# A hybrid decoder layer on one core: loading the input, placing the query work, and ordering seven products

## The chip, the core and the metric

The kernel runs on one NeuronCore of a Trainium2 chip. The engines are TensorE (PE in the profile, with its weight loads as PEld), VectorE (DVE), ScalarE (ACT), GpSimd (POOL) and SyncE (SP, which here only issues DMAs). The metric is the device time of one execution in microseconds; the median of three runs counts.

## The reference, cut to what matters

```python
xn = rmsnorm(x, norm1_w)
proj = xn @ w_in                    # q | k,v of three branches | gates | xr | yr | merge gates
q = rope_partial(rmsnorm(q, q_norm_w), t)
o_nsa = nsa_mixer(q, ...)           # compressed, selected and window attention
xc = conv_b + sum(xp[:, j:j + S] * conv_w[j] for j in range(4))
o_lru = rg_lru(xc) * gelu(yr)       # gates, scan over the sequence
merged = sigmoid(g_a) * (o_nsa @ w_nsa_up) + sigmoid(g_b) * (o_lru @ w_lru_up)
h = x + merged @ w_o
out = h + square(relu(rmsnorm(h, norm2_w) @ w_ff1)) @ w_ff2
```

The sequence has 1024 tokens, the model width is 1024, the hidden layer of the last two products is 4096 wide. All data are float32.

## The kernel before

Every float32 product is made of three passes with the operands split into a high part (`h`, by ACT) and a low part (`l` = value minus high part, by DVE): h·h, h·l and l·h. So each operand costs one ACT and one DVE instruction before PE can use it, and a matmul of 512 columns is issued three times for each 128x128 block.

The order of instructions on each engine is fixed when the program is built. The text gives a priority; the builder goes through modelled time and gives an engine that would be free the ready instruction of the highest priority, so an instruction can come ahead of an earlier one that is not ready. `high_priority(200)` raises what is inside by 200 places. Tiles come from pools with a fixed number of slots (`bufs`); a tile waits for a free slot.

The stages, in order:

- **Head** (lines 255 to 322). x comes transposed, in eight blocks of 128x1024 (`x_load(k)`, 512 KB, with the block `ar` of the attention weights, 175 KB). Three slots hold x, so block 3 is loaded when block 0 has been used. For each k, ACT and DVE make `xh`, `xl`, `ah`, `al`; PE adds 18 matmuls of 350 columns (six token tiles, three passes) into six accumulators `acc`. ACT also squares the block, and POOL adds the squares up in `accsq` (the tile `rbc`), which later gives the norm of each token.
- **Attention projections** (`ac`), then the compressed keys (`kc`, `phi`), and eight rounds j of the recurrent branch (from line 736): `fx`, a convolution on DVE (`lru_conv`), its split (`lru_split`), gates (`pg`), `fy`, a scan. `q_proc` is a generator that works on one of eight query tiles per step: a DVE multiply (L558), a POOL multiply (L559) and, one step later, four-line rotary work on DVE (L426 to L428). Each round ends with one step of it.
- **Attention** with the merge gates (`fg`) filled in between, the up-projections, and `wo`.
- **First feed-forward product** (`f1`). A 2x2 scheme with seven products for each of 16 column groups g (Strassen-Winograd). Products 1 and 2 of the groups 0 to 7 run first (`f1e`, `EARLY = 8`). The rest is a list, `FORD = product_order(16)`. A product is 12 matmuls. `PROD` names for each product the PSUM bank, `a`, `b` or `c`, that it adds into. For one g the products 6, 5 and 3 add into the same bank `a` and its value is taken out after each one (`ff_keep(g, "U2")` after 6, `ff_keep(g, "U4")` after 5), so the next of the three must wait for that copy. `ff_prep` makes the weight side of the product that stands two places ahead in the list (sums S1 to S4 on DVE, then the split), at high priority; `ff_raw` holds two raw tiles for each g, with slots for two g. `u_combos` makes the sums of the activations that the second product needs and stores them in HBM (`d_u`).
- **Second feed-forward product**: seven passes of 16 steps (`PASS`, `steps`). `f2_load` loads for each step a weight tile (`K` or `wr`) and an activation tile (`ur`) of 256 KB each, and `f2_prep` splits them. The `K` tiles share the 40 slots of pool `xb` with the activation sides (`comb`) of products 6, 7, 5, 3 and 4. Activation tiles, sums and results share 28 slots (`vt`).

The list before (g, product), for a group g from 1 to 6: (g,6) (g,7) (g,5) (g,3) (g,4); from g = 7 on, (g+1,1) (g+1,2) stand between (g,5) and (g,3).

Of the kernel before, what the change touches and what calls it, by code (L numbers as in the profile page):

```python
# [10 lines left out]
F32 = mybir.dt.float32  # L11
F32R = mybir.dt.float32r
AF = mybir.ActivationFunctionType
OP = mybir.AluOpType
# [3 lines left out]
P = 128  # L18
S = 1024
D = 1024  # L20
NK = 8
# [4 lines left out]
AW = 350  # L26
KCOFF = 4 * S
RESERVE = 2
EARLY = 8
PAD = 32  # L30
WAVE = 1
WPRI = 200
NFILL = 3
XFILL = 12
# [57 lines left out]


def product_order(n):
    out = [(g, p) for p in (6, 7, 5) for g in range(WAVE)]
    for g in range(WAVE - 1):
        out += [(g, 3), (g, 4)]
    for g in range(WAVE - 1, n):
        if g >= WAVE:
            out += [(g, 6), (g, 7), (g, 5)]  # L100
        if g + 1 < n and g + 1 >= EARLY:
            out += [(g + 1, 1), (g + 1, 2)]
        out += [(g, 3), (g, 4)]
    return out

# [29 lines left out]
def layer_kernel(ctx, tc, xT, w_att, w_lru, w_nsa, w_ff2, stream, rows, small, phi_w2, consts, masks, outT, scratch=None):  # L137
    nc = tc.nc
    V, A, G, T = nc.vector, nc.scalar, nc.gpsimd, nc.tensor

    pools = Pools(tc)
# [120 lines left out]
    rbc = xp.tile([P, S], F32, name="rbc")  # L262

    wa = pools.open("wa", side="right")
    xs_p = pools.open("xs_p", bufs=3, side="left")
    psT = pools.open("psT", side="left", space=PSUM)
    psA = pools.open("psA", side="left", space=PSUM)

    def attw_load(c, k):
        raw = wa.tile([P, AW], F32, name=f"ar{c}_{k}", tag="ar", bufs=4)  # L270
        nc.sync.dma_start(raw, w_att[c, :, k])
        return raw

# [10 lines left out]
    def x_load(k):  # L284
        t = xs_p.tile([P, S], F32, name=f"xs{k}", tag="xs")
        if k == 0:
            araw[(0, k)] = attw_load(0, k)
            for hs in HS:
                nc.sync.dma_start(t[:, hs], xT[0:P, hs])
        else:  # L290
            nc.sync.dma_start(t, xT[k * P:(k + 1) * P, :])
            araw[(0, k)] = attw_load(0, k)
        xs.append(t)

    nc.sync.dma_start(sm, small)
    for k in range(3):
        x_load(k)
    make_identity(nc, ident)
    G.memset(ones2, 1.0)
# [3 lines left out]
    for k in range(NK):  # L303
        if k == 0:
            aw[(0, k)] = attw_split(araw.pop((0, k)), 0, k)
        for hs in HS if k == 0 else [slice(0, S)]:
            A.activation(xh[k][:, hs], xs[k][:, hs], AF.Copy, scale=smc("n1", k))
            V.scalar_tensor_tensor(xl[k][:, hs], xs[k][:, hs], smc("n1", k), xh[k][:, hs].bitcast(F32), op0=OP.mult, op1=OP.subtract)
        if k:
            aw[(0, k)] = attw_split(araw.pop((0, k)), 0, k)  # L310
        if k == 0:
            A.activation(accsq, xs[k], AF.Square)
        else:
            sq = xs_p.tile([P, S], F32, name=f"sq{k}", tag="sq", bufs=2)
            A.activation(sq, xs[k], AF.Square)
            G.tensor_tensor(accsq, accsq, sq, op=OP.add)
        if k + 3 < NK:
            x_load(k + 3)
        for t in range(6):
            ts = slice(t * P, (t + 1) * P)  # L320
            mm3(acc6[t][:, :AW], xh[k][:, ts], xl[k][:, ts], *aw[(0, k)], k == 0, k == NK - 1)

    aw_iter = iter([(c, k) for c in (1, 2) for k in range(NK)])
    aw_ld = iter([(c, k) for c in (1, 2) for k in range(NK)])
# [349 lines left out]
    def lru_split(j):  # L674
        s = lst[j]
        s["h"] = lt("xch", j, S, F32R)
        s["l"] = lt("xcl", j, S, F32R)
        A.activation(s["h"], s["xc"], AF.Copy)
        V.tensor_tensor(s["l"], s["xc"], s["h"].bitcast(F32), op=OP.subtract)

    def lru_gates(j):
        h, l = lw.pop(j)
# [52 lines left out]
    for j in range(8):  # L735
        if j == 4:
            w = ws_get("vc")
            for half in range(2):
                cjob(psB, "vc", half, w, 5)
                step()  # L740
            phi["zz"] = phi_prep("v", 0)
        w = ws_get("xr")
        xy = lt("xr", j, S + P)
        xr = xy[:, 0:S + 3]
        G.memset(xr[:, 0:3], 0.0)
        for half in range(2):
            ps = ftile(psB, f"fx{j}{half}", 5)
            fjob(ps, HS[half], w)
            if half:
                ws_done()  # L750
            V.tensor_tensor(xr[:, 3 + half * 512:515 + half * 512], ps, rbc[:, HS[half]], op=OP.mult)
            if half == 0:
                step()
                if j:
                    lru_gates(j - 1)
        lru_conv(j, xr)
        lru_one(j - 1)
        lru_split(j)
        lru_root(j - 1)
        lw_prep(j)  # L760
        step()
        for i in PHI_AT[j]:
            phi_piece(i)
        w = ws_get("yr")
        y = xr[:, 3:S + 3]
        lst[j]["y"] = y
        for half in range(2):
            ps = ftile(psB, f"fy{j}{half}", 5)
            fjob(ps, HS[half], w)
            V.tensor_tensor(y[:, HS[half]], ps, rbc[:, HS[half]], op=OP.mult)  # L770
            if half:
                ws_done()
            else:
                lru_end(j - 1)
                step()
                step()
        step()
        next(q_gen, None)
    lru_gates(7)
    next(q_gen, None)  # L780
    drain()
# [427 lines left out]
    FORD = product_order(16)  # L1209
    ff = {"prep": 0, "w": {}, "raw": {}, "ps": {}, "sv": {}}  # L1210
    uq = {}

    def ff_raw(g):
        if g not in ff["raw"]:
            n = st["prepped"]
            assert order[n] == ("f1", g), (order[n], g)
            while st["loaded"] < min(len(order), n + 4):
                ws_load()
            ff["raw"][g] = (st["raw"].pop(n), st["raw"].pop(n + 1))
            st["prepped"] += 2  # L1220
            st["next"] += 2
        return ff["raw"][g]

    def ff_prep():
        if ff["prep"] >= len(FORD):
            f2_prep()
            return
        g, p = FORD[ff["prep"]]
        ff["prep"] += 1
        with tc.high_priority(WPRI):  # L1230
            ra, rb = ff_raw(g)
            a11, a12, a21, a22 = ra[:, 0:512], ra[:, 512:1024], rb[:, 0:512], rb[:, 512:1024]
            sv = ff["sv"].setdefault(g, {})

            def comb_w(name, x, y, op):
                t = vt(f"{name}_{g}")
                V.tensor_tensor(t, x, y, op=op)
                sv[name] = t
                return t

            if p == 1:
                src = a11
            elif p == 2:
                src = a12
            elif p == 6:
                src = comb_w("S2", comb_w("S1", a21, a22, OP.add), a11, OP.subtract)
            elif p == 7:
                src = comb_w("S3", a11, a21, OP.subtract)
            elif p == 5:
                src = sv["S1"] if g >= WAVE else comb_w("S1b", a21, a22, OP.add)  # L1250
            elif p == 3:
                s2 = sv["S2"] if g >= WAVE else comb_w("S2b", comb_w("S1c", a21, a22, OP.add), a11, OP.subtract)
                src = comb_w("S4", a12, s2, OP.subtract)
            else:
                src = a22
            ff["w"][(g, p)] = split_w(src, f"f{g}_{p}")
# [52 lines left out]
    def ff_product(g, p):  # L1309
        _, bn, bank = PROD[p]  # L1310
        first = p in (2, 7) or p == (6 if g < EARLY else 1)
        if first:
            ff["ps"][(g, bank)] = fps(f"p1{bank}{g}")
        ps = ff["ps"][(g, bank)]
        ff_mm(ps, ff["w"].pop((g, p)), bn, first, p in (2, 3, 4))
        ff_prep()
        ff_done(g, p, ps)
        if p == 3 and g < EARLY:
            t = uq[(g, 0, 0)] = vt(f"ub{g}")
            r = (UC["B11"] * 16 + g) * P  # L1320
            nc.sync.dma_start(t, d_u[r:r + P, :])
        if p == 4:
            u_combos(g, False)
            if g == 15:
                u_combos(g, True)
        if p == 6 and g:
            u_combos(g - 1, True)
        if g == 15:
            f2_load()

# [28 lines left out]
    def f2_load():  # L1359
        n = f2["loaded"]  # L1360
        if n >= len(steps) or n - f2["prepped"] >= LDA:
            return
        f2["loaded"] += 1
        pi, k = steps[n]
        p = PASS[pi][0]
        hi, f = {1: (0, k), 7: (1, k), 6: (1, k + 16), 4: (1, k + 16), 5: (0, k), 2: (0, k + 16), 3: (0, k + 16)}[p]
        if p == 1:
            w = f2["K"][k] = xb_tile(f"K{k}").bitcast(F32)
        else:
            w = vt(f"wr{p}{k}")  # L1370
        nc.sync.dma_start(w, w_ff2[f * P:(f + 1) * P, HS[hi]])
        u = vt(f"ur{p}{k}")
        r = (pi * 16 + k) * P
        nc.sync.dma_start(u, d_u[r:r + P, :])
        f2["raw"][n] = (w, u)

    def f2_prep():
# [29 lines left out]
    for g in range(EARLY):  # L1407
# [5 lines left out]
            if g == 0 and p == 1:  # L1413
                stats2(1, acc, sq)
        ws_done()
        if g == EARLY - 1:
            ff_prep()
            ff_prep()
        if g < 4:
            for c in (g, g + 4):  # L1420
# [147 lines left out]
```

## Time and profile before

| what | value |
|---|---|
| median of 3 runs | 1628.48 us (1627.82 to 1628.57) |
| profiled execution | 1626.14 us, of which the span from the first to the last instruction is 1624.3 us |
| PE busy | 1574.7 us (97%) |
| DVE busy | 1115.6 us (69%) |
| ACT busy | 849.9 us (52%) |
| POOL busy | 309.8 us (19%) |
| mean granted TensorE clock | 0.993 of full speed |

A row of the profile that begins with a time gives the start, the duration, the engine, the line in the kernel, the operation and the tile written and read; a bracket at the end is the time the engine sat idle before, and what ended it. `PEclk` is the granted TensorE clock of a stretch as a share of full speed (1.0 is 2.4 GHz, 0.5 is 1.2 GHz). PE can be busy and yet slow: matmul durations double at the lower clock.

### The profile page before, as it was taken

Reading aid. Unit: us, or ns where it says so; the run is one execution under the profiler, and the core shown is the slowest. Engines: PE = TensorE matmul, PEld = TensorE weight load, DVE = VectorE, ACT = ScalarE, POOL = GpSimd, SP = SyncE. Lnnn points to the kernel's source line nnn. Section 1 sums busy time; section 2 is a strip of 40 time slices with the busy share of each in tenths; the row PEclk is TensorE's granted clock in tenths of the full one; section 3 lists DMA queues with packets and bytes.
Section 4 is the critical chain, followed back from the end, with each engine's and each line's share of the span. In section 5 each row is a group of like instructions: output and inputs, shape, how many; then the busy total and the mean of one; then the engine's idle time right before and its main releaser. Section 6 shows DMA issues by size and latency. Waiting matters only on the chain.

```text
span 1624.3 us, 21975 instructions
## 1 busy us (share of the span) xinstructions
PE 1574.7 (97%) x7541; PEld 1316.1 (81%) x7541; DVE 1115.6 (69%) x2124; ACT 849.9 (52%) x1570; POOL 309.8 (19%) x421
## 2 busy tenths in 40 slices
PE   6998999999999999999999999899999999999999
PEld 6997788887888887887788888777888878888887
DVE  8639778775888878886544448877666678657571
ACT  5442675765667656675533345644455554444440
POOL 4002212222334444332000221022111210000000
PEclk9999999999999999999999999999999999999999
DMA  5211222222101211114532554355444499457750
GB/s 192 66 31 43 69 84 80 85 90 97 49 30 34 63 59 39 34 33 152 195 120 101 194 182 149 110 206 181 171 155 149 141 356 327 155 187 232 236 187 26
DMA packets 86688, 206.80 MB, mean 127 GB/s; under 512 B 11184, under 2 KB 15792, under 8 KB 86576
## 3 DMA queue, kind: packets, MB, share of 16 engines
q1 hardware_dynamic: 71856, 157.15, 28.9%
q0 software_dynamic: 14720, 48.25, 8.2%
q8 instruction: 59, 0.97, 0.3%
q14 instruction: 53, 0.43, 0.1%
HBM read 152.93 MB, written 52.43 MB: 126 GB/s over the span
## 4 chain that ended last, share of the span: by engine, by line
PE 68%; DVE 2%; issue 2%; DMA 2%; ACT 2%; POOL 1%; ACTq 0%; POOLq 0%; DVEq 0%
PE p L1466 6%; PE p L1467 6%; PE p L1465 6%; PE pt L948 3%; PE p1a L1305 3%; PE p1a L1307 3%; PE p1a L1306 3%; PE fg L236 3%; PE fg L240 3%; PE fg L238 3%; PE po L236 2%; PE po L240 2%; PE po L238 2%; PE p1c L1305 2%; PE p1c L1306 2%
## 5 line engine op out<-in xcount | busy, mean ns | idle before, releaser
L1467 PE MATMUL p<-hu,lw 128*128 128x512 f32 x448 | 174.4, 389 | 0.0
L1466 PE MATMUL p<-lu,hw 128*128 128x512 f32 x448 | 174.4, 389 | 0.0
L1465 PE MATMUL p<-hu,hw 128*128 128x512 f32 x448 | 174.4, 389 | 0.0
L203 DVE TENSOR_TENSOR wl<-wr,wh 128x512 fp32r<-128x512 f32 x156 | 113.5, 733 | 86.4 <-ACT wh L202 81.1
L202 ACT ACTIVATE wh<-wr 128x512 fp32r<-128x512 f32 x156 | 97.0, 627 | 132.8 <-PE po L238 40.8
L1141 ACT ACTIVATE hu<-ur 128x512 fp32r<-128x512 f32 x112 | 69.5, 629 | 155.2 <-PE p L1466 148.7
L953 ACT ACTIVATE ph<-pt 128x512 fp32r<-128x512 f32 x148 | 87.9, 595 | 86.5 <-PE pt L948 85.3
L954 DVE TENSOR_TENSOR pl<-pt,ph 128x512 fp32r<-128x512 f32 x148 | 101.8, 688 | 27.1 <-ACT ph L953 25.1
L1142 DVE TENSOR_TENSOR lu<-ur,hu 128x512 fp32r<-128x512 f32 x112 | 76.9, 690 | 62.6 <-ACT hu L1141 60.7
L236 PE MATMUL fg<-xh,wh 128*128 128x512 f32 x256 | 111.6, 436 | 5.1 <-DVE ge L794 4.8
L240 PE MATMUL fg<-xh,wl 128*128 128x512 f32 x256 | 102.0, 398 | 0.0
L238 PE MATMUL fg<-xl,wh 128*128 128x512 f32 x256 | 101.3, 396 | 0.0
L1465 PEld LDWEIGHTS p<-hu,hw 128*128 128x128 f32 x448 | 84.1, 188 | 17.6
L1467 PEld LDWEIGHTS p<-hu,lw 128*128 128x128 f32 x448 | 84.1, 188 | 17.5
L1466 PEld LDWEIGHTS p<-lu,hw 128*128 128x128 f32 x448 | 84.1, 188 | 17.3
L1288 ACT ACTIVATE z<-z 128x512 f32<-128x512 f32 x56 | 35.4, 632 | 77.0 <-DVE z L1287 76.1
L203 DVE TENSOR_TENSOR wlf<-S,whf 128x512 fp32r<-128x512 f32 x63 | 42.2, 691 | 31.5 <-ACT whf L202 31.4
L1260 POOL DMA_DIRECT2D d_u<-z x48 | 25.9, 540 | 182.5 <-ACT z L1263 181.6
L236 PEld LDWEIGHTS fg<-xh,wh 128*128 128x128 f32 x256 | 48.8, 191 | 14.1 <-issue 3.5
L240 PEld LDWEIGHTS fg<-xh,wl 128*128 128x128 f32 x256 | 48.4, 189 | 10.7
L236 PE MATMUL fy<-xh,wh 128*128 128x512 f32 x128 | 51.3, 400 | 3.8 <-ACT wh L202 3.7
L976 PE MATMUL o<-ph,V 128*128 128x512 f32 x132 | 54.2, 411 | 0.0
(860 smaller groups left out, 4599.9 us busy)
## 6 DMA issues: line engine op xcount, KB each, us to landing
wr<-in_stream SPq DMA_DIRECT2D x106, 512.0 KB, 3.5
ur<-d_u SPq DMA_DIRECT2D x112, 256.0 KB, 4.4
wr<-in_w_ff SPq DMA_DIRECT2D x96, 256.0 KB, 4.1
d_u<-uT POOLq DMA_DIRECT2D x64, 256.0 KB, 3.2
d_u<-z POOLq DMA_DIRECT2D x48, 256.0 KB, 2.8
d_gm<-ge POOLq DMA_DIRECT2D x32, 256.0 KB, 2.6
g<-d_gm SPq DMA_DIRECT2D x32, 256.0 KB, 2.8
ar<-in_w_att SPq DMA_DIRECT2D x24, 175.0 KB, 2.9
```

The costliest lines, as they stand in the source:

```text
L202: A.activation(h, src, AF.Copy)
L203: V.tensor_tensor(l, src, h.bitcast(F32), op=OP.subtract)
L236: T.matmul(ps, h[:, b], mh[k0 + k][:, sl], start=(k == 0), stop=False)
L238: T.matmul(ps, h[:, b], ml[k0 + k][:, sl], start=False, stop=False)
L240: T.matmul(ps, l[:, b], mh[k0 + k][:, sl], start=False, stop=(k == nk - 1))
L953: A.activation(ph, pst, AF.Copy)
L954: V.tensor_tensor(pl, pst, ph.bitcast(F32), op=OP.subtract)
L1305: T.matmul(ps, h[:, b], bh, start=first and k == 0, stop=False, skip_group_check=True)
L1306: T.matmul(ps, h[:, b], bl, start=False, stop=False, skip_group_check=True)
L1465: T.matmul(ps[d], wh[:, b], uh, start=fresh and kk == 0, stop=False, skip_group_check=True)
L1466: T.matmul(ps[d], wh[:, b], ul, start=False, stop=False, skip_group_check=True)
L1467: T.matmul(ps[d], wl[:, b], uh, start=False, stop=kk == 15, skip_group_check=True)
```

## The change

Five edits. (1) The slots for x and its weight blocks become eight, so that all loads are issued at the start; the squares are made in place after the loop over k in the text, and DVE adds them instead of POOL. (2) The DVE part of each step of `q_proc` may not be issued before the last DVE instruction of that round's `lru_split`. (3) The list of products: (g,6) comes ahead of (g-1,3) (g-1,4), and (g,7) (g,5) behind them; the last two groups end with (14,3) (14,4) (15,3) (15,4). The sums S1 and S2 are no longer made twice for g = 0. The first `ff_prep` comes one group earlier (after g = 6 instead of two after g = 7). (4) `u_combos` of a group is called one product later, all four sums together. (5) The loads of the second product are kept in the order of the text.

```diff
--- before.py
+++ after.py
@@ -28,7 +28,6 @@
 RESERVE = 2
 EARLY = 8
 PAD = 32
-WAVE = 1
 WPRI = 200
 NFILL = 3
 XFILL = 12
@@ -92,16 +91,15 @@
 
 
 def product_order(n):
-    out = [(g, p) for p in (6, 7, 5) for g in range(WAVE)]
-    for g in range(WAVE - 1):
-        out += [(g, 3), (g, 4)]
-    for g in range(WAVE - 1, n):
-        if g >= WAVE:
-            out += [(g, 6), (g, 7), (g, 5)]
+    out = []
+    for g in range(n):
+        out.append((g, 6))
+        if 0 < g < n - 1:
+            out += [(g - 1, 3), (g - 1, 4)]
+        out += [(g, 7), (g, 5)]
         if g + 1 < n and g + 1 >= EARLY:
             out += [(g + 1, 1), (g + 1, 2)]
-        out += [(g, 3), (g, 4)]
-    return out
+    return out + [(g, p) for g in (n - 2, n - 1) for p in (3, 4)]
 
 
 
@@ -262,12 +260,12 @@
     rbc = xp.tile([P, S], F32, name="rbc")
 
     wa = pools.open("wa", side="right")
-    xs_p = pools.open("xs_p", bufs=3, side="left")
+    xs_p = pools.open("xs_p", bufs=NK, side="left")
     psT = pools.open("psT", side="left", space=PSUM)
     psA = pools.open("psA", side="left", space=PSUM)
 
     def attw_load(c, k):
-        raw = wa.tile([P, AW], F32, name=f"ar{c}_{k}", tag="ar", bufs=4)
+        raw = xs_p.tile([P, AW], F32, name=f"as{k}", tag="as") if c == 0 else wa.tile([P, AW], F32, name=f"ar{c}_{k}", tag="ar", bufs=4)
         nc.sync.dma_start(raw, w_att[c, :, k])
         return raw
 
@@ -293,7 +291,7 @@
         xs.append(t)
 
     nc.sync.dma_start(sm, small)
-    for k in range(3):
+    for k in range(NK):
         x_load(k)
     make_identity(nc, ident)
     G.memset(ones2, 1.0)
@@ -308,17 +306,16 @@
             V.scalar_tensor_tensor(xl[k][:, hs], xs[k][:, hs], smc("n1", k), xh[k][:, hs].bitcast(F32), op0=OP.mult, op1=OP.subtract)
         if k:
             aw[(0, k)] = attw_split(araw.pop((0, k)), 0, k)
-        if k == 0:
-            A.activation(accsq, xs[k], AF.Square)
-        else:
-            sq = xs_p.tile([P, S], F32, name=f"sq{k}", tag="sq", bufs=2)
-            A.activation(sq, xs[k], AF.Square)
-            G.tensor_tensor(accsq, accsq, sq, op=OP.add)
-        if k + 3 < NK:
-            x_load(k + 3)
         for t in range(6):
             ts = slice(t * P, (t + 1) * P)
             mm3(acc6[t][:, :AW], xh[k][:, ts], xl[k][:, ts], *aw[(0, k)], k == 0, k == NK - 1)
+
+    for k in range(NK):
+        A.activation(xs[k], xs[k], AF.Square)
+        if k == 1:
+            V.tensor_tensor(accsq, xs[0], xs[1], op=OP.add)
+        elif k:
+            V.tensor_tensor(accsq, accsq, xs[k], op=OP.add)
 
     aw_iter = iter([(c, k) for c in (1, 2) for k in range(NK)])
     aw_ld = iter([(c, k) for c in (1, 2) for k in range(NK)])
@@ -676,7 +673,7 @@
         s["h"] = lt("xch", j, S, F32R)
         s["l"] = lt("xcl", j, S, F32R)
         A.activation(s["h"], s["xc"], AF.Copy)
-        V.tensor_tensor(s["l"], s["xc"], s["h"].bitcast(F32), op=OP.subtract)
+        s["last"] = V.tensor_tensor(s["l"], s["xc"], s["h"].bitcast(F32), op=OP.subtract)
 
     def lru_gates(j):
         h, l = lw.pop(j)
@@ -775,7 +772,8 @@
                 step()
                 step()
         step()
-        next(q_gen, None)
+        with tc.issue_after(lst[j]["last"].ins):
+            next(q_gen, None)
     lru_gates(7)
     next(q_gen, None)
     drain()
@@ -1209,6 +1207,7 @@
     FORD = product_order(16)
     ff = {"prep": 0, "w": {}, "raw": {}, "ps": {}, "sv": {}}
     uq = {}
+    uc = []
 
     def ff_raw(g):
         if g not in ff["raw"]:
@@ -1218,7 +1217,6 @@
                 ws_load()
             ff["raw"][g] = (st["raw"].pop(n), st["raw"].pop(n + 1))
             st["prepped"] += 2
-            st["next"] += 2
         return ff["raw"][g]
 
     def ff_prep():
@@ -1247,10 +1245,9 @@
             elif p == 7:
                 src = comb_w("S3", a11, a21, OP.subtract)
             elif p == 5:
-                src = sv["S1"] if g >= WAVE else comb_w("S1b", a21, a22, OP.add)
+                src = sv["S1"]
             elif p == 3:
-                s2 = sv["S2"] if g >= WAVE else comb_w("S2b", comb_w("S1c", a21, a22, OP.add), a11, OP.subtract)
-                src = comb_w("S4", a12, s2, OP.subtract)
+                src = comb_w("S4", a12, sv["S2"], OP.subtract)
             else:
                 src = a22
             ff["w"][(g, p)] = split_w(src, f"f{g}_{p}")
@@ -1319,12 +1316,13 @@
             t = uq[(g, 0, 0)] = vt(f"ub{g}")
             r = (UC["B11"] * 16 + g) * P
             nc.sync.dma_start(t, d_u[r:r + P, :])
+        while uc:
+            u_combos(*uc.pop(0))
         if p == 4:
-            u_combos(g, False)
+            uc.extend([(g, False), (g, True)])
             if g == 15:
-                u_combos(g, True)
-        if p == 6 and g:
-            u_combos(g - 1, True)
+                while uc:
+                    u_combos(*uc.pop(0))
         if g == 15:
             f2_load()
 
@@ -1368,10 +1366,10 @@
             w = f2["K"][k] = xb_tile(f"K{k}").bitcast(F32)
         else:
             w = vt(f"wr{p}{k}")
-        nc.sync.dma_start(w, w_ff2[f * P:(f + 1) * P, HS[hi]])
+        tc.keep_in_program_order(nc.sync.dma_start(w, w_ff2[f * P:(f + 1) * P, HS[hi]]))
         u = vt(f"ur{p}{k}")
         r = (pi * 16 + k) * P
-        nc.sync.dma_start(u, d_u[r:r + P, :])
+        tc.keep_in_program_order(nc.sync.dma_start(u, d_u[r:r + P, :]))
         f2["raw"][n] = (w, u)
 
     def f2_prep():
@@ -1413,8 +1411,7 @@
             if g == 0 and p == 1:
                 stats2(1, acc, sq)
         ws_done()
-        if g == EARLY - 1:
-            ff_prep()
+        if g >= EARLY - 2:
             ff_prep()
         if g < 4:
             for c in (g, g + 4):
```

## Rows read from the trace of the kernel before

**Rows 1.** Busy by stretch: from:to, length, engines' busy (count), PEclk, DMA share, GB/s.
```profile
10.00:12.00 2.00, 1.17 (x7) 0.88 (x6) 2.00 (x3) 2.00 (x3) 0.80 (x1) 1.00 0.94 355
...
14.73:42.83 28.10, 19.43 (x109) 19.13 (x108) 27.77 (x33) 14.89 (x22) 15.66 (x6) 0.88 0.51 167
26.80:42.80 16.00, 15.15 (x94) 14.85 (x93) 15.94 (x16) 8.90 (x14) 7.62 (x3) 1.00 0.66 217
141.40:155.00 13.60, 8.64 (x26) 6.46 (x25) 13.51 (x22) 3.34 (x6) 1.65 (x1) 0.75 0.20 66
171.40:361.00 189.60, 189.12 (x877) 157.53 (x877) 144.00 (x179) 127.48 (x158) 37.23 (x26) 1.00 0.23 80
1034.95:1048.93 13.98, 10.32 (x37) 7.74 (x36) 12.07 (x20) 6.22 (x11) 0.54 (x1) 0.88 0.16 57
1048.93:1138.00 89.07, 83.29 (x361) 67.12 (x360) 68.65 (x109) 39.77 (x66) 19.31 (x36) 1.00 0.55 192
```

**Rows 2.** What PE waited for over the whole span: us in total, times, longest.
```profile
PE acc L228 <- DVE al L278: 9.5, 3, 7.8
PE p1a L1305 <- DVE U L1295: 6.1, 7, 0.9
...
PE fy L236 <- ACT wh L202: 3.7, 1, 3.7
PE p1a L1305 <- ACT whf L202: 3.2, 1, 3.2
...
PE fx L236 <- DVE xr L751: 2.5, 1, 2.5
```

**Rows 3.** Head, PE in order of time: longest wait, end of head.
```profile
22.56 0.66 PE L228 MATMUL acc<-al,xh 128*128 128x350 f32 x1 [7.82 <-DVE al L278]
...
42.83 0.33 PE L227 MATMUL ac<-ah,xh 128*128 128x350 f32 x1
```

**Rows 4.** Head, DVE in order of time.
```profile
11.02 0.52 DVE L278 TENSOR_TENSOR al<-ar,ah 128x350 fp32r<-128x350 f32 x1
...
18.65 1.27 DVE L308 SCALAR_TENSOR_TENSOR xl<-xs,sm,xh 128x1024 fp32r<-128x1024 f32 x1
19.85 2.66 DVE L278 TENSOR_TENSOR al<-ar,ah 128x350 fp32r<-128x350 f32 x1
```

**Rows 5.** Head, POOL in order of time (four adds merged).
```profile
11.20 10.92 POOL L316 TENSOR_TENSOR rbc<-rbc,sq 128x1024 f32<-128x1024 f32 x4 [9.89 <-ACT sq L315]
```

**Rows 6.** Head, ACT in order of time: the second and the sixth block of x.
```profile
8.63 1.15 ACT L307 ACTIVATE xh<-xs,sm 128x1024 fp32r<-128x1024 f32 x1 [0.66 <-DMA xs<-in_xT]
...
23.38 1.15 ACT L307 ACTIVATE xh<-xs,sm 128x1024 fp32r<-128x1024 f32 x1 [5.14 <-DMA xs<-in_xT]
```

**Rows 7.** Line 679: count, ns min/median/max, first and last start, form.
```profile
L679 DVE TENSOR_TENSOR xcl<-xc,xch x8: 1215/1222/1228, 159.1 to 356.8; 128x1024 fp32r<-128x1024 f32 x8
```

**Rows 8.** Busy time of the query tiles' instructions alone (DVE, ACT, POOL).
```profile
126.00:141.40 15.40, 7.67 (x10) 0.00 (x0) 7.56 (x5) 1.00 0.10 35
```

**Rows 9.** Line 559, the POOL multiply of a query tile.
```profile
L559 POOL TENSOR_TENSOR yq<-yq,rowq x8: 1283/1634/1737, 127.0 to 164.5; 128x512 f32<-128x512 f32 x8
```

**Rows 10.** Start of the listed products, DVE in order of time.
```profile
1035.75 0.68 DVE L1237 TENSOR_TENSOR S<-wr 128x512 f32<-128x512 f32 x1
```

**Rows 11.** Raw weight tiles, 1045 to 1300 us: time from issue to landing.
```profile
DMA to landing us min/median/max: 3.1/4.8/6.3
```

**Rows 12.** Near 1300 us: SP, ACT, PE by time; then a stretch as in Rows 1.
```profile
1296.86 2.37 SPq L1371 DMA_DIRECT2D K<-in_w_ff  x5
...
1307.61 0.63 ACT L1141 ACTIVATE hu<-ur 128x512 fp32r<-128x512 f32 x1 [3.40 <-DMA ur<-d_u]
...
1309.29 0.50 PE L1305 MATMUL p1a<-hB,whf 128*128 128x512 f32 x1 [3.85 <-ACT U L1297]
...
1309.30:1312.00 2.70, 2.70 (x8) 0.65 1.04 394
```

## The prediction

> **What bounds the kernel now.** I read busy time by stretch first. PE is the bound nearly everywhere: 189.1 of 189.6 us in the recurrent rounds, so only PE's holes can be gained, and what the lower clock costs behind them [rows 1]. The table of PE's waits then names the holes [rows 2], and the order of time in each stretch says why the named engine was late. Five places carry nearly all that the five edits touch: the head, 141 to 155 us, a wait of 2.5 us on L751, the start of the listed products at 1035 us, and the copies between products of one bank (one a group, and the last at 1305 us).
>
> **Head (edit 1).** PE waits 7.82 us for one `al` [rows 3]. That DVE instruction takes 0.52 us at k = 1 and 2.66 us at 19.85, while POOL adds squares without a break from 11.20 to 22.12 [rows 4, 5]. So the POOL adds stretch DVE's instructions with two inputs. The second cause is the three slots: at 23.38 us ACT had sat 5.14 us for the sixth block [rows 6]. Both go: POOL has nothing left in the head, and no load waits for a slot.
>
> What bounds the head then? Loads: 512 + 175 KB for a k at 355 GB/s [rows 1] is 2.0 us. Block 1 is there at 8.63 us [rows 6], so block 7 at about 20.5. PE: 26.80 to 42.80 holds 94 matmuls in 15.15 busy us, 0.161 us each [rows 1]. The wait of 7.82 us that ends at 22.56 begins at 14.74, where k = 0 and 1 are done; six k of 18 matmuls take 17.4 us more, so the head ends at 32.1 instead of 42.83 [rows 3]. DVE: after `al` of k = 1 (11.5 us) it owes six times 1.27 + 0.52 = 10.7 us [rows 4], seven adds of 1024 columns, priced by the two-input L679 at 1.22 us, 8.5 us [rows 7], and some 3 us of small ones (the constants of the recurrence; an estimate: they run in the same stretch): it is through at 33.7. If all adds came ahead of the last `al`, the last k would end near 36. The adds stand behind the loop in the text, hence at the lowest priority there, so I take 33.0: **9.8 us gained** (6.8 to 10.7).
>
> **Query work (edit 2).** From 126 to 141.4 us DVE spends 7.67 us on query tiles and POOL 7.56 beside it [rows 8]. Behind that stretch `fy` waits 3.7 us for `wh` [rows 2]: ACT, in order, sits on the splits of `zt`, which DVE made late. 141.40 to 155.00 holds 26 matmuls; at the 0.231 us that follow from 83.29 us for 361 [rows 1] they need 6.0, so 7.6 us are lost, part as idle time, part at a clock of 0.75. Without 7.67 us of query work ahead of it, `zt` is ready before PE needs it. The wait of 2.5 us on `xr` L751 [rows 2] sits behind five tiles of rotary work and goes too. **7.6 + 2.5 = 10.1 us gained** (6 to 10.1).
>
> What is late next: the same work now falls on the eight rounds. A tile costs DVE 7.67 / 5 = 1.5 us, and up to the 1.64 us of its POOL multiply if a DVE instruction meets it [rows 9]. DVE is busy 144 of 189.6 us there [rows 1], so seven rounds have 6.5 us each free, twice the 3.1 us. Nothing waits for the query tiles until attention. Lower end 0; upper end, each tile's 3.1 us on the path in half of the rounds, 12 us. The nearest row is the wait of 2.5 us, which came from five tiles in a heap; one tile alone is a fifth of that, 0.5 a round, and not in each: **1.5 us lost**. The Trainium skill (SBUF — State Buffer, Who interferes with whom) says that a DVE instruction with two SBUF inputs and a POOL one that reads SBUF exclude each other for a whole instruction, whichever came second waiting it out. By that rule all eight POOL multiplies could cost DVE their full 1.64 us, 13.1 in all, and with all of it on the path the time would be some 1606.6 instead; the `al` of 2.66 us in the head agrees with the rule [rows 4, 5].
>
> **Start of the listed products (edit 3, its `ff_prep`).** 1034.95 to 1048.93 holds 36 matmuls (37 records), 8.3 us of work in 14.0: 5.7 us lost, with 3.2 of them as a wait for `whf` and the rest mostly at the lower clock [rows 1, 2]. The sum S1 that this weight needs runs at 1035.75 [rows 10], after products 1 and 2 are all done, though its inputs are weights. It takes a slot of `vt`, and behind it in time only activation tiles of the group before give slots free. One group earlier in the text means some 5.5 us (24 matmuls) earlier for S1 and S2, before PE arrives. S3 for the second product follows at once and may still be about 1 us late. **4.7 us gained** (0 to 5.7). The double S1 and S2 dropped (three DVE instructions) are off PE's path.
>
> **Order of the products (edit 3).** Before, (g,3) follows (g,5) on bank `a` and waits for the copy U4: 6.1 us in 7 waits [rows 2], g = 0 to 6. Now (g+1,6) lies between, 12 matmuls or 2.8 us, against 0.9. The same holds between 6 and 5 (three products between) and 6 after 1 (one). **6.0 us gained** (5 to 7). At the end, (15,3) waited 3.85 us for U4 on ACT, because ACT sat 3.40 us on an `ur` load that queued with `K` loads [rows 12]; the next matmuls ran at a clock of 0.65, 2.70 us for 8 [rows 12], 0.85 more than at full clock. Now (14,3) and (14,4), 5.5 us, lie between, and the `K` slots come free two products earlier relative to their use. **4.7 us gained** (1 to 5.5).
>
> What is late next: raw tiles. The pair for g + 2 can be loaded when (g,4) has its weights, two places ahead of it. From the start of (g,3), four products or 11 us remain until (g+2,6) (before: six). Landing takes 3.1 to 6.3 us [rows 11], then two sums and a split, about 2.7 us at 0.68 apiece [rows 10]: 9.0 at worst. Covered, with 2 us to spare: **0.5 us lost** for the odd group.
>
> **Edits 4 and 5.** `u_combos` moves four DVE sums and four POOL stores per group by one product; DVE has 20.4 us free in 89.1 there [rows 1], and the passes that read the sums run much later. Keeping the loads in order issues each `ur` behind its own `K` instead of behind five `K` [rows 12]; its worth is inside the 4.7 above. The cost, if an `ur` without a free slot holds back the next `K`, is bounded by the landing times, 6.3 us once. Zero taken for both; if their cover went, the DVE sums would cost PE at most 2.7 us at the end.
>
> **Sum.** 9.8 + 10.1 + 4.7 + 6.0 + 4.7 = 35.3 gained, 2.0 lost: 33.3. The profiled execution took 1626.14, so 1592.8; the median of the runs stands 2.3 above it: **1595.0 us** rounded.
>
> **Rivals.**
> 1. *The early loads share the bandwidth.* Sixteen loads in flight could all land near the end, 20.5 us; PE would stand still from about 10, then work 7 k of 2.9 us, with a cold start of about 2: the head ends near 43, nothing gained there, total 1605. For it: landing times vary from load to load [rows 11]. Against it: block 1 landed at 8.63 with three more loads issued behind it by the code. The Trainium skill (DMA: Bandwidth & Descriptors, Queues, rings and completion order) has each engine take descriptors in ring order within one queue, which would exclude it; that trace row agrees. Chance 0.07.
> 2. *The query tiles stall the rounds.* Half of the tiles' cost on the path, 12 us instead of 1.5: 1605.5. For it: the wait on L751 shows that DVE in a heap stops PE. Against it: 6.5 us free in a round. Chance 0.10.
> 3. *The edits in the feed-forward part do little*: S1 still waits for a slot, ACT still sits on a load ahead of U4. 4.7 + 4.7 are not gained: 1604.5. For it: slots, not the text's place, may set S1's time. Chance 0.13.
> 4. *Slower:* the raw tiles. If the pair for g + 2 lands later than 11 - 2.7 = 8.3 us after the slot is free, PE stops in each of 14 groups; from 2.4 us a group (14 x 2.4 = 33.6) the kernel is no faster, so from a landing of 10.7 us. At 13 us: 14 x 4.7 = 66 us, less 33, total 1661. For it: `ur` loads with many others queued are that late, ACT's wait shows it. Against it: at most 6.3 us in this stage. Chance 0.03.
> 5. *Nothing comes of it*, since the new order trades each wait for another of its size (slots of `vt`, with two groups' sums alive at a time). About 1628. Chance 0.02.
>
> **Numbers.** The forecast has 0.65. Its own range follows from the bounds above: gains 40.0 at best without losses, 1588.4; about 24 with rivals 2 and 3 in part, 1604. For 8 in 10 the range takes in rivals 1 to 3 one at a time and ends below two of them together (1615): 1586 to 1608, the lower end with 2 us for holes elsewhere that shift. A change under 0.2% (3.3 us) can't be told from none here. Faster 0.95, same 0.02, slower 0.03.
>
> **What would show it.** Head: the first `ac` matmul at 32 to 34 us, no `al` over 0.6 us, POOL empty until then. 141 us: no wait of PE for `wh`, clock 1.0. Rounds: PE's idle time in the eight rounds under 2 us. Listed products: the wait for `whf` under 1 us, no wait for U, period of a group 13.9 us rather than 14.7. Near the end: no wait for U4, clock 1.0. I am wrong if DVE instructions between 180 and 360 us show up as PE's releasers with more than 5 us in sum, if raw tiles do in the products, or if the head ends after 37.

## The result, and the profile after

The changed kernel takes 1591.06 us (median of four runs, 1590.64 to 1591.7) against 1628.53 for the kernel before beside it: a ratio of 0.9769, 95% interval 0.9752 to 0.9786, so 37.5 us gained. The forecast was 1595.0 with a range of 1586 to 1608. The profiled execution took 1590.64 us, 35.5 less than the one before; its span is 1588.9 us.

PE was the bound and still is, so I read the same views again: first what PE waited for (total us, times, longest). This is the changed kernel over its whole span.

```profile
PE acc L225 <- ACT xh L305: 5.3, 1, 5.3
PE fg L234 <- DVE ge L792: 4.8, 5, 3.1
PE pt L946 <- POOL Pw L914: 2.8, 6, 1.0
PE fx L234 <- DVE xr L748: 2.5, 2, 2.1
PE acc L226 <- DVE al L276: 0.7, 1, 0.7
...
PE p1c L1302 <- ACT whf L200: 0.2, 1, 0.2
```

Of the five entries in [rows 2], four are gone or nearly so: the wait for U has no row any more, that for the `wh` of `fy` neither, `whf` is down from 3.2 to 0.2 us, and `al` from 9.5 to 0.7. One entry did not shrink: `fx` still waits 2.5 us for `xr`, now L748, but elsewhere, as will be seen. Next the stretches that answer to [rows 1], with the columns given there:

```profile
14.73:32.08 17.35, 17.35 (x111) 17.35 (x109) 17.32 (x22) 15.28 (x23) 0.00 (x0) 1.00 0.60 217
130.60:144.20 13.60, 13.60 (x62) 11.29 (x61) 13.48 (x20) 4.86 (x7) 0.20 (x1) 1.00 0.23 77
171.40:343.00 171.60, 168.31 (x778) 139.45 (x777) 145.41 (x183) 115.96 (x143) 43.10 (x31) 1.00 0.23 81
1018.20:1032.20 14.00, 13.75 (x60) 10.76 (x59) 13.44 (x22) 8.60 (x16) 0.65 (x2) 1.00 0.31 112
1032.20:1120.00 87.80, 87.80 (x389) 72.72 (x388) 73.02 (x117) 44.23 (x74) 20.61 (x39) 1.00 0.56 201
1261.10:1282.80 21.70, 21.70 (x97) 17.98 (x96) 15.76 (x26) 15.39 (x29) 4.47 (x9) 1.00 0.92 331
```

- Head: from 14.73 us PE has no hole until the attention projections begin at 32.08, instead of at 42.83 [rows 3]: 10.75 us gained. POOL is at 0.00.
- The stretch that began at 141.4 us holds 62 matmuls instead of 26 in the same 13.60 us, at a clock of 1.00 instead of 0.75. At 13.60 / 62 = 0.22 us apiece, 36 more are 7.9 us.
- Start of the listed products: 60 matmul records in 14.0 us instead of 37 in 13.98: 23 x 0.23 = 5.3 us.
- Groups after it: 389 in 87.80 us (0.226 each) instead of 361 in 89.07 (0.247): over 361 matmuls 7.6 us. Idle time makes up 5.8 of them (89.07 less 83.29); the rest is that a matmul took 0.231 busy us before and 0.226 after.
- End of the first product: no idle time and clock 1.00 into the passes, where PE had waited 3.85 us and lost 0.85 more at 0.65 [rows 12]: 4.7 us.
- The rounds are the one place that got worse: PE stands still for 3.29 of 171.60 us, against 0.48 of 189.60.

With the old wait on L751 (2.5) the gains are 38.8 us; the new waits for `xr` take 2.5 back, and the attention stretch, which no edit is aimed at, takes 2.0 more: from the first `fg` matmul to the first `p1e` 629.6 us instead of 627.6, with the clock at 0.83 near 600 us (last section). That leaves 34.3 of the 35.5 us explained. The rest lies in the feed-forward part: from the first `p1e` matmul to the end of the span 635.2 us became 616.6, 18.7 less, where the lines above give 17.6. Some 0.4 of it are the lower clock at the end of the first product, which lasted longer than [rows 12] shows: 1312 to 1314 us holds 7 matmuls at 0.62.

### The profile page after: what moved, and what is told of

Read it like the earlier page. It is cut to its first block, busy times and chain, and to the rows that moved or that the text cites. A ratio compares the mean times of both kernels' runs of the same rounds, so it can differ in the third digit from the quotient of the medians.

```text
span 1588.9 us, 21949 instructions
## 1 busy us (share of the span) xinstructions
PE 1566.3 (99%) x7541; PEld 1312.3 (83%) x7541; DVE 1112.0 (70%) x2128; ACT 854.5 (54%) x1570; POOL 290.2 (18%) x414
## 4 chain that ended last, share of the span: by engine, by line
PE 69%; issue 2%; ACT 2%; DVE 2%; DMA 1%; POOL 1%; ACTq 0%; DVEq 0%; POOLq 0%
PE p L1462 6%; PE p L1464 6%; PE p L1463 6%; PE pt L946 3%; PE p1a L1303 3%; PE p1a L1304 3%; PE p1a L1302 3%; PE fg L234 3%; PE fg L236 3%; PE fg L238 3%; PE p1c L1304 2%; PE po L234 2%; PE po L238 2%; PE po L236 2%; PE p1c L1303 2%
## 5 line engine op out<-in xcount | busy, mean ns | idle before, releaser
L201 DVE TENSOR_TENSOR wl<-wr,wh 128x512 fp32r<-128x512 f32 x156 | 110.3, 711 | 84.8 <-ACT wh L200 79.5
L952 DVE TENSOR_TENSOR pl<-pt,ph 128x512 fp32r<-128x512 f32 x148 | 101.7, 687 | 27.7 <-ACT ph L951 25.9
L1464 PEld LDWEIGHTS p<-hu,lw 128*128 128x128 f32 x448 | 84.1, 188 | 17.6
L1139 ACT ACTIVATE hw<-wr 128x512 fp32r<-128x512 f32 x64 | 39.5, 625 | 35.9 <-DVE wr L1395 17.1
```

What stands on the lines that cost most here:

```text
L201: V.tensor_tensor(l, src, h.bitcast(F32), op=OP.subtract)
L952: V.tensor_tensor(pl, pst, ph.bitcast(F32), op=OP.subtract)
L1139: A.activation(h, src, AF.Copy)
L1464: T.matmul(ps[d], wl[:, b], uh, start=False, stop=kk == 15, skip_group_check=True)
```

## Experiments

Each kernel was timed in five rounds beside the kernel before on the same chip. The theory was that the five losses are separate places with a cause each. The rivals were that one edit's lead is swallowed by the next hole, or that an edit works for another reason than the one given.

### The head: slots or POOL?

The prediction gave two causes, the POOL adds and the three slots. Three kernels, all built on the kernel before, take them apart. **Edit 1 alone:**

> The kernel before with edit 1 alone. Theory (the five losses are separate, each edit gives back its own): the first `ac` matmul moves from 42.83 to about 32.1 us as in the changed kernel, and all of the 10.7 us arrive at the end: ratio 0.9934, about 1617.8 us. Rival (the holes that stay swallow the lead, since the query work behind the head is late for reasons of its own): under 5 us arrive, above 1623.

1617.24 us, ratio 0.9932 (0.992 to 0.9944): 10.9 us gained, the first `ac` matmul at 31.76. The lead arrives whole: in the profile it is 11.1 us at this matmul and still 11.1 at the first `fg` matmul behind the rounds (350.36 instead of 361.46). **Slots alone:**

```diff
-    xs_p = pools.open("xs_p", bufs=3, side="left")
+    xs_p = pools.open("xs_p", bufs=NK, side="left")
...
-    for k in range(3):
+    for k in range(NK):
         x_load(k)
...
             G.tensor_tensor(accsq, accsq, sq, op=OP.add)
-        if k + 3 < NK:
-            x_load(k + 3)
```

> The kernel before with eight slots and all loads issued at the start; the squares stay in the loop and POOL adds them. Theory (POOL's adds stretch DVE's two-input instructions and hold the two tiles of squares): DVE's `al` still take up to 2.7 us, the first `ac` comes at 36 to 41 us, 2 to 7 us gained. Rival (the three slots are the cause): first `ac` at or below 34, 9 to 10.7 us gained.

1636.98 us, ratio 1.0053 (1.0041 to 1.0065): 8.8 us **slower** than before, which neither theory had. The first `ac` comes at 46.96. DVE by time in that head (start, duration, line, operation, tile, shape):

```profile
10.62 0.52 DVE L278 TENSOR_TENSOR al<-as,ah 128x350 fp32r<-128x350 f32 x1
11.05 2.38 DVE L473 TENSOR_TENSOR lhp<-lhp,lz 128x8 f32<-128x8 f32 x1
13.47 0.17 DVE L474 TENSOR_SCALAR lhp<-lhp 128x8 f32<-128x8 f32 x1
13.68 2.22 DVE L473 TENSOR_TENSOR lhp<-lhp,lz 128x8 f32<-128x8 f32 x1
15.93 0.17 DVE L474 TENSOR_SCALAR lhp<-lhp 128x8 f32<-128x8 f32 x1
16.14 2.20 DVE L473 TENSOR_TENSOR lhp<-lhp,lz 128x8 f32<-128x8 f32 x1
18.26 1.27 DVE L308 SCALAR_TENSOR_TENSOR xl<-xs,sm,xh 128x1024 fp32r<-128x1024 f32 x1
19.45 2.67 DVE L278 TENSOR_TENSOR al<-as,ah 128x350 fp32r<-128x350 f32 x1
22.05 2.35 DVE L474 TENSOR_SCALAR lhp<-lhp 128x8 f32<-128x8 f32 x1
...
24.64 2.25 DVE L474 TENSOR_SCALAR lhp<-lhp 128x8 f32<-128x8 f32 x1
...
27.12 2.21 DVE L474 TENSOR_SCALAR lhp<-lhp 128x8 f32<-128x8 f32 x1
29.25 1.27 DVE L308 SCALAR_TENSOR_TENSOR xl<-xs,sm,xh 128x1024 fp32r<-128x1024 f32 x1
```

And POOL beside it, the seven adds merged, then their least, median and longest duration in ns:

```profile
10.80 18.50 POOL L316 TENSOR_TENSOR rbc<-rbc,sq 128x1024 f32<-128x1024 f32 x7 [9.49 <-ACT sq L315]
L316 POOL TENSOR_TENSOR rbc<-rbc,sq x7: 2362/2402/3355, 10.8 to 26.9; 128x1024 f32<-128x1024 f32 x7
```

With all blocks there, ACT runs ahead with the squares and POOL adds seven times without a break. During these seven adds exactly seven DVE instructions take 2.2 to 2.7 us each, and their size doesn't matter: an instruction on **eight columns** (L473, 0.16 us when POOL is idle) takes as long as one on 350. Three of the seven (L474) read one tile only. It goes the other way too: the add of 3.36 us starts at 18.39, behind DVE's `xl` of 18.26, which kept its 1.27. The small constants of the recurrence, which I had counted as 3 us in all, stand in DVE's order ahead of the `xl` of k = 2; five of them took from 11.05 to 18.3, and PE waited for the `al` behind. The three slots had held POOL back, and so had protected DVE: in the kernel before, POOL stood still for 3.88 us from 22.12 on, and the constants that DVE ran then took 0.16 to 0.17 us.

```profile
26.00 3.03 POOL L316 TENSOR_TENSOR rbc<-rbc,sq 128x1024 f32<-128x1024 f32 x1 [3.88 <-ACT sq L315]
```

The head accounts for only 4.1 us of the loss. As much again arises in the rounds, where PE's one wait for `xr` grew from 2.5 to 4.7 us: in this kernel's order a rotary line (L424) stands ahead of that `xr`, meets a POOL multiply of `li` and takes 2.44 us, and the 4 us behind the wait run at a clock of 0.57 instead of 1.00. **DVE's adds alone**, with three slots:

```diff
-            G.tensor_tensor(accsq, accsq, sq, op=OP.add)
+            V.tensor_tensor(accsq, accsq, sq, op=OP.add)
```

> The kernel before, three slots and squares in the loop, but DVE adds them. Theory (POOL is the cause, and through the late squares also of the late slots): no `al` over 0.6 us, first `ac` at 34 to 37 us, 6 to 9 us gained. Rival (the three slots are the cause): ACT still waits some 5 us for the sixth block, first `ac` at 39 or later, under 4 us gained.

1619.31 us, ratio 0.9946 (0.9934 to 0.9957): 8.9 us gained, the first `ac` at 32.00. The long wait of ACT for a block [rows 6] is gone with three slots as well:

```profile
15.96 1.14 ACT L307 ACTIVATE xh<-xs,sm 128x1024 fp32r<-128x1024 f32 x1
...
18.81 1.16 ACT L307 ACTIVATE xh<-xs,sm 128x1024 fp32r<-128x1024 f32 x1 [0.38 <-DMA xs<-in_xT]
...
21.20 1.14 ACT L307 ACTIVATE xh<-xs,sm 128x1024 fp32r<-128x1024 f32 x1
```

So the wait that I read as a lack of slots was POOL's too: late adds kept the two tiles of squares, ACT's squares waited for these, and the slots came free late. One word in one line ends the head at 32.00 us; the eight slots bring 0.24 us more. The 2.1 us between the two medians don't come from the head: the profiles are 0.3 us apart at the first `fg` matmul (350.36 and 350.70) and 1.7 at the first `p1e` (980.87 and 982.56), in the stretch whose length varies from profile to profile (last section).

### The query work

**Edit 2 alone**, on the kernel before:

```diff
-        V.tensor_tensor(s["l"], s["xc"], s["h"].bitcast(F32), op=OP.subtract)
+        s["last"] = V.tensor_tensor(s["l"], s["xc"], s["h"].bitcast(F32), op=OP.subtract)
...
-        next(q_gen, None)
+        with tc.issue_after(lst[j]["last"].ins):
+            next(q_gen, None)
```

> The kernel before with edit 2 alone. Theory: the stretch behind 141 us gives back 8.1 us and the wait on the first tile of a later round 2.5, and the new wait in the round at some 268 us takes 2.1: 8.5 us gained, about 1620 us, no wait of PE for `wh` of `fy`. Rival (the wait for `wh` comes from the splits' own place, or the lead of the head made the stretch clean in the changed kernel): a wait for `wh` of over 2 us stays and under 4 us are gained.

1619.67 us, ratio 0.995 (0.9938 to 0.9963): 8.5 us gained. The stretch of 141.4 to 155 us is full, and the waits for `wh` of `fy` are gone; PE's waits for `xr` L751 are 2.5 us in two, the longer 2.1:

```profile
141.40:155.00 13.60, 13.60 (x63) 11.29 (x63) 13.48 (x20) 5.01 (x7) 0.00 (x0) 1.00 0.24 77
```

The wait of 2.1 us is the new one; in the changed kernel it ends at 268.0 us. DVE by time there:

```profile
260.56 0.68 DVE L767 TENSOR_TENSOR xr<-fy,rbc 128x512 f32<-128x512 f32 x1
261.16 1.88 DVE L423 TENSOR_TENSOR rpq<-yq,qcon 128x128 f32<-128x128 f32 x1
262.96 0.68 DVE L555 TENSOR_TENSOR yq<-yq,facq 128x512 f32<-128x512 f32 x1
263.57 0.28 DVE L424 TENSOR_TENSOR yq<-yq,qcon 128x128 f32<-128x128 f32 x1
263.77 1.72 DVE L590 TENSOR_TENSOR zt<-cn_t,sm 64x252 f32<-64x252 f32 x1
...
267.27 0.69 DVE L748 TENSOR_TENSOR xr<-fx,rbc 128x512 f32<-128x512 f32 x1
```

and POOL:

```profile
260.13 2.76 POOL L714 TENSOR_TENSOR li<-li,xr 128x1024 f32<-128x1024 f32 x1 [16.61 <-DVE li L713]
...
263.80 1.30 POOL L556 TENSOR_TENSOR yq<-yq,rowq 128x512 f32<-128x512 f32 x1
```

A query step falls together with the sums of `zt` there, and its first rotary line takes 1.88 us instead of 0.29 because it meets POOL's multiply of `li`. Three kernels, on the changed one, take this apart. The step left out in one round is made up in the last:

```diff
-            next(q_gen, None)
+            for _ in range((1, 1, 1, 1, 1, 0, 1, 2)[j]):
+                next(q_gen, None)
```

> The changed kernel with no query step in the round j = 5 and two in the last round. In j = 5 the query step falls together with the sums of `zt` (L590), and PE's matmuls `fx` waited 2.1 us for `xr` L748. Theory (the query step makes DVE late there): the wait is gone, 2.1 us gained, about 1589 us. Rival (the sums of `zt` alone make it late): the wait stays, no change; or the two steps of the last round bring a wait of their own.

1590.06 us; the wait stays at 2.1. This was the wrong round, and says nothing on the cause. With the zero at j = 4, `(1, 1, 1, 1, 0, 1, 1, 2)`:

> The changed kernel with no query step in the round j = 4 and two in the last; the run before left it out in j = 5, and the step that falls together with `zt` at 261 us is that of j = 4, by the fifth of the `xcl` instructions (L676) at 256.04 us. Theory: the wait of 2.1 us for `xr` is gone and arrives at the end, 2 us gained (some 1588.5 to 1589). Rival (four sums of `zt` alone make DVE late): the wait stays above 1 us.

1587.49 us (1585.78 to 1588.3), ratio 0.975 (0.9737 to 0.9764). The wait is 0.3 us, and 260 to 270 us is full (the changed kernel has 7.87 of 10 there):

```profile
260.00:270.00 10.00, 10.00 (x46) 8.18 (x45) 8.23 (x12) 6.29 (x8) 4.26 (x4) 1.00 0.29 107
```

The step was what made DVE late; the sums of `zt` alone fit. Now the multiply of L556 on DVE instead:

```diff
-            G.tensor_tensor(yq[t], yq[t], rowq, op=OP.mult)
+            V.tensor_tensor(yq[t], yq[t], rowq, op=OP.mult)
```

> The changed kernel with the second multiply of a query tile (L556) on DVE instead of POOL. Theory (the rotary line L423 is stretched to 1.88 us by POOL's multiply of `li`, L714, and only one sum of `zt` by the query multiply): L423 stays at 1.88 us, `zt` falls from 1.72 to 0.58, DVE gets 0.68 us more; the wait of 2.1 us for `xr` becomes some 1.6, the time stays within 1 us. Rival (the query multiply on POOL is what stretches DVE): L423 falls to 0.3 us, the wait goes, 2.1 us gained.

1588.57 us, ratio 0.9763 (0.9749 to 0.9776). By DVE's order of time in this kernel L423 stays long and `zt` is short, as the theory had it:

```profile
260.36 1.89 DVE L423 TENSOR_TENSOR rpq<-yq,qcon 128x128 f32<-128x128 f32 x1
...
262.98 0.68 DVE L556 TENSOR_TENSOR yq<-yq,rowq 128x512 f32<-128x512 f32 x1
...
263.79 0.57 DVE L590 TENSOR_TENSOR zt<-cn_t,sm 64x252 f32<-64x252 f32 x1
```

The wait fell to 1.6 us; the median is 2.5 below the changed kernel's, more than the half microsecond of the theory, and outside the 1 us that was expected. Last, the changed kernel again beside the one with both edits, on one chip:

> The changed kernel itself once more, as the measure for the next one on the same chip: 1591 us within 1.5, and with the matmuls near 600 us at a clock of 0.83 again, if that drop belongs to the kernel's timing (theory), or at 1.00, if it comes and goes from run to run (rival).

> The changed kernel with no query step in the round j = 4 and two in the last, and with the second multiply of a query tile on DVE. Theory (both remove the one wait for `xr` at 267 us, which the shift alone has taken to 0.3): no more than the shift alone, 1587 to 1588, 2.5 to 4 us under the changed kernel. Rival (POOL's multiplies also cost DVE in other places that count): 1586 or less.

1590.10 us (1589.38 to 1590.95) and 1586.86 (1585.62 to 1589.08). The clock near 600 us was at 1.00 this time, as the rival had it (last section). The two ranges don't meet, so the version with both edits is 3.2 us better than the changed kernel; that both are better than the move alone can't be said from the times. The profiles say a little more, with one execution each: the first `fg` matmul behind the rounds comes at 342.4 to 343.3 us in five profiles with the changed kernel's rounds, at 341.4 with the multiply moved, at 340.2 with the step moved and at 339.4 with both.

### The first feed-forward product

On the changed kernel, **`ff_prep` started as before:**

```diff
-        if g >= EARLY - 2:
+        if g == EARLY - 1:
+            ff_prep()
             ff_prep()
```

> The changed kernel with `ff_prep` started as before, twice after g = 7. Theory (the place in the text sets when S1 is made, and 36 matmuls then need 14.0 us instead of 8.3): the wait for `whf` is back with some 3 us, 5 to 5.7 us lost, about 1596.5 us. Rival (the other edits, the new list or the later sums, free the slots of `vt` and would have made S1 early anyway): under 1.5 us lost.

1595.42 us, ratio 0.9783 (0.9769 to 0.9798): 4.4 us above the changed kernel. The wait for `whf` is back with 3.2 us, and so is the stretch:

```profile
1017.00:1031.00 14.00, 10.75 (x35) 8.22 (x35) 11.91 (x20) 6.68 (x12) 0.54 (x1) 0.76 0.14 46
```

35 records against 60: 25 x 0.23 = 5.8 us, more than the medians show, whose difference is uncertain by some 3 us. The profiles settle it: from the first `p1e` matmul to the end of the span the changed kernel takes 616.6 us in both its profiles, and so do the four kernels above that differ from it only in the rounds; this one takes 622.5, 5.9 more. The place in the text sets when S1 is made: 46.7 us after the first `p1e` matmul here and in the kernel before, 41.5 in the changed kernel. **The list of before**, and beside it the kernel that is its control, with **the loads of the second product free**:

```diff
-        tc.keep_in_program_order(nc.sync.dma_start(w, w_ff2[f * P:(f + 1) * P, HS[hi]]))
+        nc.sync.dma_start(w, w_ff2[f * P:(f + 1) * P, HS[hi]])
...
-        tc.keep_in_program_order(nc.sync.dma_start(u, d_u[r:r + P, :]))
+        nc.sync.dma_start(u, d_u[r:r + P, :])
```

> The changed kernel with the list of products of before, and with the loads of the second product free in their order (the old list can't be combined with the fixed order of loads). To be held against the next one, which has the free loads alone. Theory: seven waits for U4 of 0.9 us are back, each over 1 us with what they cost behind them (7.3 in all), and at the end a wait for U4 with matmuls at a clock of 0.65 behind it (5.7): 10 to 13 us lost, 1601 to 1604. Rival (the later sums `u_combos` were what made room): under 4 us lost.

> The changed kernel with the loads of the second product free in their order. Theory (the new list alone took the wait for U4 away from the end, as 24 matmuls stand between (15,5) and (15,3)): within 1.5 us of the changed kernel. Rival (ACT sits on a late `ur` and what PE needs from ACT is late with it): a wait of PE for ACT of 2 us or more near 1270 us, 3 to 5.5 us lost.

With free loads alone 1591.87 us (1591.01 to 1593.24): by the times edit 5 can't be told from nothing. From the first `p1e` matmul on this profile takes 617.7 us, 1.2 more than the changed kernel, and PE has a wait of 0.5 us for `whf` that isn't there otherwise. With the old list as well 1605.83 (ratio 0.985, 0.9834 to 0.9867), 14.0 us above that. PE's waits of that kernel from 1015 to 1300 us:

```profile
PE p1a L1303 <- DVE U L1293: 8.9, 7, 1.6
PE p1a L1303 <- ACT U L1295: 2.2, 1, 2.2
PE p1c L1303 <- ACT whf L201: 0.2, 1, 0.2
```

and its stretch behind the last of them:

```profile
1288.00:1292.00 4.00, 4.00 (x12) 3.15 (x13) 2.77 (x6) 3.22 (x6) 0.43 (x1) 0.63 1.05 399
```

The list alone makes and removes the waits for U: 8.9 + 2.2, and at a clock of 0.63 behind the last one 12 matmuls stand where others of 4 us hold 18 or 19, 1.4 us. That is 12.5; the medians say 14.0, with an uncertainty of some 3 us for such a difference, and from the first `p1e` matmul on the profiles say 13.8 (631.5 and 617.7).

## Why the prediction was right, and where it was not

By the times the edits are worth 10.9 (edit 1 alone), 8.5 (edit 2 alone), 4.4 (`ff_prep`), 14.0 (the list) and 0.8 us (the loads): 38.6 against 37.5 measured, with 2 to 3 us of uncertainty in each. Edit 4 was not run by itself. The profiles are sharper. Up to the first `fg` matmul edits 1 and 2 gain 11.1 and 7.8 us alone and 18.8 together, so these losses were separate and nothing was swallowed. Behind the first `p1e` matmul `ff_prep`, the list and the loads are worth 5.9 + 13.8 + 1.2 = 20.9 one at a time, and everything together 18.7: some 2 us there count twice.

- **Head.** 9.8 forecast, 10.75 measured. The bound named, 18 matmuls per k by PE, gave 32.1 and was met at 32.08; the allowance up to 33.0 for DVE's adds wasn't needed. DVE has 17.32 busy us in the 17.35 of that stretch and still isn't late: three of the seven adds run ahead of the last `al`, which ends at 25.9 us, and PE begins with that k at 29.2. The step that failed is "the second cause is the three slots". They were a result of the first cause, and giving more slots with POOL still adding costs 8.8 us. Had the change been only that, I would have forecast its sign wrongly, as the expectation for that run did. "Instructions with two inputs" was too narrow as well: three of the stretched ones read one tile.
- **Query work.** 10.1 forecast; 7.9 behind 141 us plus the wait of 2.5 on L751. The price was 1.5, spread thinly over rounds, and came as 2.5, 2.1 of it in one round. The mechanism I used (a fifth of a heap of five tiles, 0.5 a round) was wrong in kind: in all the other rounds together PE waited once more, for 0.4 us, and the one in which a step met POOL's `li` and the four sums of `zt` paid the rest, before what the clock costs behind it. "DVE has 6.5 us free in a round" was true of the round and not of the 6 us before `xr`. Idle PE time under 2 us was named as the mark for the rounds; it was 3.3.
- **Start of the listed products.** 4.7 forecast with 1 us left for S3; 5.3 gained, `whf` waits 0.2.
- **Order of the products.** 6.0 forecast in the groups; 7.6 by the matmul rate, since each wait of 0.9 us also costs a slow start behind it (1.8 of the 7.6). 4.7 at the end, met by [rows 12], 5.1 with the lower clock up to 1314 us. The raw tiles (0.5) never released PE.
- **The rivals.** Shared bandwidth fell: the `al` of k = 1 came at 11.32 us against 11.02 [rows 4], and no later block stopped PE. Query tiles at 12 us fell to 2.5. The rule of the Trainium skill (SBUF — State Buffer, Who interferes with whom) was that a DVE instruction with two SBUF inputs and a POOL one that reads SBUF exclude each other for a whole instruction. The run with slots alone agrees for four of its seven stretched DVE instructions (2.20 to 2.67 us, two inputs each) and for the POOL add of 3.36 us; the rule as quoted doesn't speak of the other three, with one input. Its sum of 13.1 us on the path didn't come: in the changed kernel the first rotary line of a tile takes 1.5 to 1.9 us for six of the eight tiles, so DVE did pay, but PE waited for `xr` only twice, 2.5 us in all. Edits that do little in the feed-forward part fell by the two runs on `ff_prep` and on the list, late raw tiles by the table of waits; the landing of 10.7 us that this rival needs is in no row, the latest `ur` near 1300 us took 9.3.

The median came out 3.9 us below the number. Of these, 2.2 are the gain (35.5 by the profiles against 33.3); nearly all the rest is that the median was taken to stand 2.3 us above the profiled execution, and stands 0.4 above it. The gain itself is nearer than its terms: some 40 us gained against 35.3, 4.5 lost against 2.0. That the errors partly cancel is luck, and the 2.0 us in the attention stretch were in no term. One sum is off: the upper ends of the gains make 39.0 us, not 40.0, so the best case is 1589.5 and not 1588.4; the range stands without it.

## What to carry to other kernels

When an instruction is slow in a profile, look at what the other engine runs at that moment before you add buffers: a wait for a free slot can be the far end of the same contention, and a tight buffer can be what limits it. Price what you move into a loop by the fullest stretch that it can fall into, not by the loop's mean idle time. A wait of PE between two products costs its length, a slow start and sometimes the clock behind it, so putting one independent product between two uses of a bank gains more than the table of waits shows.

## What had not been expected of the hardware

DVE instructions that meet POOL pay by the piece, not by size: eight columns cost 2.2 to 2.4 us beside POOL's adds of 1024 columns (2.40 us in the median), and 0.16 us without.

The fall of the clock behind a short hole isn't a property of the kernel. The changed kernel, run twice, has the same hole of 2.13 us, which ends at 267.9 or 268.0 us. The stretch behind it in its second profile, and then in its first:

```profile
268.00:272.00 4.00, 4.00 (x11) 3.15 (x12) 2.70 (x5) 3.99 (x6) 0.39 (x1) 0.57 0.01 4
```

```profile
268.00:272.00 4.00, 3.98 (x17) 3.30 (x18) 2.80 (x5) 3.99 (x6) 0.28 (x1) 1.00 0.02 4
```

11 matmuls against 17: 6 x 0.23 = 1.4 us, in one execution and not in the other. Not all of it reaches the end of the rounds: the first `fg` matmul comes 0.65 us later (343.34 and 342.69). At 600 us it is the reverse: the first profile of the changed kernel and then its second:

```profile
600.00:610.00 10.00, 9.50 (x42) 7.77 (x43) 6.19 (x17) 5.30 (x13) 3.10 (x5) 0.83 0.00 1
```

```profile
600.00:610.00 10.00, 9.04 (x50) 7.43 (x50) 7.32 (x20) 6.37 (x15) 3.54 (x6) 1.00 0.00 1
```

From the first `fg` matmul to the first `p1e` the first profile takes 629.6 us and the second 627.7; the run with free loads, the same kernel up to there, takes 631.3. Over all fourteen profiles this stretch runs from 627.6 to 631.9 us, though no edit is aimed at it. So a wait that an edit removes can be worth its length in one profile and one or two us more in another, and a difference of up to some 4 us between the spans of two profiles says nothing here by itself; the stretch that an edit touches has to be compared alone. What decides where the clock falls isn't shown by these runs.
